# Layer 1's mixer works on an input that is not normalized: rstd moves into the Gelus, half of v into Strassen's products, and the FFNs' rstd is laid out later

## The chip, the core and the metric

The kernel runs on one core of a Trainium2 chip. The metric is the device time of one execution in microseconds. A core has five engines that run side by side, each with its own queue in order: TensorE (matmuls; the profile calls it PE, and its loads of the stationary operand PEld), VectorE (DVE), ScalarE (ACT), GpSimd (POOL) and SyncE (SP), which issues DMAs here. Matmuls write into PSUM, which has eight banks of 512 float32 columns; VectorE and ScalarE move results from there to SBUF. Engines wait for one another on semaphores.

## The reference, cut to what matters

A decoder trunk of two layers on 512 tokens with 1024 channels, in float32. In layer 0 the mixer is a gated short convolution and a causal pooling; in layer 1 it is a chunked spatial gating:

```python
xn = rms_norm(h, norm_mix[1])                # h * rstd(token) * gain(channel)
proj = gelu(xn @ w_in_odd)                   # 1024 -> 2048, exact Gelu
u, v = proj[..., :1024], proj[..., 1024:]
mix = chunked_spatial_gating(u, v, ...)      # vn = rms_norm(v); gate over 128 positions; u * gate
h = h + mix @ w_out_odd
```

After each mixer comes a gated convolutional FFN of width 2816: `g` and `up` are products of the normalized input, `g` goes through a causal convolution of width 3, and `silu(g) * up` is multiplied by `w_ffn_down`. The rstd of an RMSNorm is one number per token. It is a factor of a whole row of `xn`, so it can as well be applied to the row of `xn @ w`.

## The kernel before, in words

**Numbers.** Each float32 operand is split into a high and a low half (`hi`, `lo`, type float32r), and a product is three matmuls (`mm3`, L153 to L156): hi x hi, hi x lo, lo x hi. The splits are the main work of ScalarE (`hi`, a copy) and VectorE (`lo`, the difference): `parts` for weights (L146), `halves` and `split` for others. `summed` (L136) makes `lo` with ScalarE and an accumulating DMA of POOL.

**Layout.** `h` is held in eight tiles of 128 channels x 512 tokens; `hg` are the halves of h times the gain, not yet times rstd. `Norm.rstd_cols` (L223) makes rstd with tokens on partitions: eight tiny matmuls of the sum of squares, then a root and a Newton step on VectorE and ScalarE (`inv_sqrt`). `Norm.rstd_spread` (L213) lays it out along the free axis: four transposes on TensorE (`ssr`) and a copy on ScalarE.

**Strassen.** The FFNs' `both` (L682) and layer 1's `InProducts` (L907) multiply 2 x 2 blocks with seven products for eight, in Winograd's form. `multiply` (L532) runs one product of 12 matmuls of 256 columns. Products 1, 6, 7 and 4 accumulate in one bank "a", 5 and 3 in "e", 2 in "b"; after a product of "a" ScalarE copies the state out of the bank before the next product adds to it. The token side needs sums of blocks (`t23`, `t41` in the FFNs, `sums` in the mixer), the weight side sums of raw weight blocks (`rest`, L922), each split again.

**Layer 1's mixer** (`mixer1`, L817). v is 512 + 512 columns of `w_in_odd`, u likewise. `v_group(0)` multiplies `hg` as it is with the first half of v's weights, plainly, with tokens as the stationary operand; its results get rstd as the scale of their Gelu (L965). Meanwhile rstd is made and laid out, at the hooks (3, 0) and (4, 2) of the group. With it `normalize(kp)` (L872), for four pairs of channel tiles, makes the normalized input, splits it into `hg` anew, and makes and splits the four block sums. `v_group(1)` multiplies the second half of v plainly with the normalized `hg`. `u0 = InProducts("u0", 0)` is Strassen's, with the block sums; the second half of u is plain (`in_group("u1", ...)`), and spatial gating runs along with it.

**The FFNs.** The first two columns of tiles (f = 0) are plain: `direct` (L605) runs triples `(i, j)`, i over eight channel tiles, j over two gate and two up tiles. At its hooks, `rstd_cols` is made at (3, 0) and `rstd_spread` at (4, 1) (L771 to L774). `block_sums` of the FFN (L635) is called after it in the program, then the results leave PSUM with rstd as a factor (L624). All later pairs f = 2, 4, ... go through `both`, with a half of the down projection between two of them (`STEPS`, L523).

**Order.** The order of the instructions on each engine is made by a planner: it takes ready work by priority, which is the order in the program, with its own estimates of durations, so instructions of later parts fill gaps of earlier ones. It does so on TensorE too. Instructions wrapped in `inorder` keep their place in TensorE's stream; `rstd_cols` and `rstd_spread` are. `behind` adds an order by hand. Buffers are rings: `raw` has four weight tiles, `whi` and `wlo` six each, PSUM seven banks for matmuls and one for others.

Of the kernel before, what the change touches and what calls it, by code (L numbers as in the profile page):

```python
# [32 lines left out]
def tile_trunk(ctx: ExitStack, tc: tile.TileContext, x, norm_mix, norm_ffn, final_norm,  # L33
# [486 lines left out]

    STEPS = [(0, None, [0]), (2, (0, 2, 0), [2]), (4, (0, 2, 1), [4])]  # L523
    for f in range(6, NF, 4):
        STEPS += [(f, (f - 4, f, 0), []), (f + 2, (f - 4, f, 1), [f, f + 2])]
    HALF = S // 2
    NP = NK // 2
    PAIRS = [k for i in range(NP) for k in (i, i + NP)]
# [25 lines left out]
    class Ffn:  # L554
# [211 lines left out]
        def hidden(self, f, before=lambda i, j: None):  # L766

            if f == 0:
                def first(i, j):
                    before(i, j)  # L770
                    if (i, j) == (3, 0):  # L771
                        nc.vector.tensor_copy(self.cols, self.norm.rstd_cols(inorder))
                    elif (i, j) == (4, 1):
                        self.r = self.norm.rstd_spread(inorder)  # L774

                ch = self.pair_weights([("g", 0), ("u", 0), ("g", 1), ("u", 1)])
                rest = self.direct(ch, first)
# [6 lines left out]
            def split_acts():  # L784
                for ft, row in rows:
                    self.act(ft, row)

            return split_acts

        def steps(self, half_down, before=lambda i, j: None):  # L790
            waiting = {}
            for f, part, ready in STEPS:
                waiting[f] = self.hidden(f, before)
                if part is not None:
                    half_down(*part)
                for done in ready:
                    waiting[done]()

    def ffn0(norm):
        nonlocal prm1  # L800
        with tc.tile_pool(name="f0", bufs=1) as ap:
            def sums(kp):
                return [ap.tile([P, 2, HALF], F32R, name=f"t23{i}_{kp}") for i in "hl"]

            ffn = Ffn(0, prm0, norm, ap, sums)
            def half_down(a, b, half):
                project(f"d0_{a}", w_ffn_down[0], ffn.acts, list(range(a, b)), None,
                        halves=(half,), tail=0)

            ffn.steps(half_down)  # L810
            prm1 = params1()
            nxt = Norm("m1", lambda k: prm1("mix", k))
            project("d0_last", w_ffn_down[0], ffn.acts, list(range(NF - 4, NF)), nxt)
            return nxt


    def mixer1(norm):  # L817
        w = w_in_odd[0]
        with tc.tile_pool(name="m1", bufs=1) as mp:
# [4 lines left out]
            def v_group(half, hooks):  # L824

                chunks = {}
                c0 = 1024 + half * 512
                for kp in range(NP):
                    raw = wp.tile([P, 2, 512], F32, tag="raw", bufs=4, name=f"raw_v{half}_{kp}")
                    nc.sync.dma_start(raw, w[:, c0 : c0 + 512].rearrange(  # L830
                        "(h k p) c -> p h k c", h=2, p=P)[:, :, kp])
                    hi, lo = parts(raw, 2, 512, f"v{half}_{kp}")
                    chunks[kp], chunks[kp + NP] = (hi[:, 0], lo[:, 0]), (hi[:, 1], lo[:, 1])
                banks = {}
                head = NK - 2
                for i, j in ([(i, j) for i in range(head) for j in range(NT)]
                             + [(i, j) for j in range(NT) for i in range(head, NK)]):
                    if (i, j) in hooks:
                        hooks[i, j]()
                    k, cs = PAIRS[i], slice(j * P, (j + 1) * P)  # L840
                    if j not in banks:
                        banks[j] = mm_bank(f"v{half}_{j}")
                    mm3(banks[j], (hg[k][0][:, cs], hg[k][1][:, cs]), chunks[k],
                        i == 0, i == NK - 1)
                return banks

            r = []
            banks = v_group(0, {(3, 0): lambda: norm.rstd_cols(inorder),
                                (4, 2): lambda: r.append(norm.rstd_spread(inorder))})

            work2 = [mp.tile([P, 2, S], F32, tag="v", bufs=4, name=f"nx{i}") for i in range(4)]
            both = mp.tile([P, 4, S], F32, tag="u", bufs=2, name="nx4")
            work2 += [both[:, :2], both[:, 2:]] * 2
            v = [mp.tile([P, D], F32, tag="v", bufs=4, name=f"v{t}") for t in range(NT)]
            ssv = mp.tile([P, 4, PAD], F32, name="ssv")[:, :, :NT]

            def v_square(half, t):
# [11 lines left out]
                nc.scalar.activation(dst[0], src, AF.Copy)  # L869
                nc.vector.tensor_tensor(dst[1], src, dst[0].bitcast(F32), ALU.subtract)  # L870

            def normalize(kp):  # L872
                x, t = work2[2 * kp], work2[2 * kp + 1]
                for i, k in enumerate((kp, kp + NP)):
                    nc.vector.scalar_tensor_tensor(x[:, i, :], h[k], prm1("mix", k), r[0],
                                                   op0=ALU.mult, op1=ALU.mult)
# [5 lines left out]
                nc.vector.tensor_tensor(t[:, 0, :], a21, a22, ALU.add)  # L882
# [18 lines left out]
            class InProducts:  # L901
# [31 lines left out]
                def run(self, out_, done):  # L933
                    banks = ({}, {})
                    e = {}
                    for i, product in ((0, 1), (1, 1), (0, 2), (1, 2), (0, 6), (1, 6), (0, 5),
                                       (0, 7), (1, 5), (1, 7), (0, 4), (0, 3), (1, 4), (1, 3)):
                        hi, lo = self.stat[product]
                        ps = multiply(banks[i], f"{self.name}_{i}", product, tokens(product, i),
                                      lambda kp: (hi[:, kp, :], lo[:, kp, :]))  # L940
                        c = {1: (0, 0), 2: (0, 0), 6: (0, 1), 3: (0, 1), 7: (1, 1), 5: (1, 1),
                             4: (1, 0)}[product]
                        dst = out_(i + 2 * c[0])[:, c[1] * HALF : (c[1] + 1) * HALF]
                        if product in (1, 6):
                            nc.scalar.copy(dst, ps)
                        elif product == 5:
                            e[i] = ps
                        elif product == 7:
                            nc.scalar.copy(dst, ps)
                            nc.vector.tensor_tensor(dst, e[i], dst, ALU.add)  # L950
                            nc.scalar.activation(dst, dst, AF.Gelu)
                        elif product == 4:
                            nc.scalar.activation(dst, ps, AF.Gelu)
                            done(i + 2)
                        else:
                            nc.vector.tensor_tensor(dst, ps, dst, ALU.add)
                        if product == 3:
                            row = out_(i)
                            nc.scalar.activation(row, row, AF.Gelu)
                            done(i)  # L960

            for kp in range(NP):
                normalize(kp)
            for t in range(NT):
                nc.scalar.activation(v[t][:, :512], banks[t], AF.Gelu,  # L965
                                     scale=norm.cols[:, t : t + 1])
                v_square(0, t)
            banks = v_group(1, {})
            for t in range(NT):
                nc.scalar.activation(v[t][:, 512:], banks[t], AF.Gelu)  # L970
                v_square(1, t)
            u0 = InProducts("u0", 0)
            u0.plain()

# [86 lines left out]
                        spatial(j + 4)  # L1061

            def u1_done(t, ps):
                nc.scalar.activation(u[1][:, t, :], ps, AF.Gelu)
# [16 lines left out]
    def ffn1(norm):  # L1081
        with tc.tile_pool(name="f1", bufs=1) as ap:
# [96 lines left out]
            ffn.steps(half_down, before)  # L1179
            last_down(NF - 4, NF)  # L1180

    def down(name, ks, pieces, lhs, rhs, on_done):
# [42 lines left out]
```

## Time and profile before

| | |
|---|---|
| median of 3 runs | 994.0 us (993.97 to 995.07) |
| profiled execution | 993.98 us, its span 992.2 us |
| granted TensorE clock | 0.999 |
| busy: PE, PEld, DVE, ACT, POOL | 980.7, 880.9, 769.4, 544.6, 99.1 us |
| matmuls | 6049 |
| DMA | 125.1 MB |

In the rows of the profile a line like `L543 PE MATMUL u_0a<-whi_u,hgh` names the line of the kernel, the engine, the operation, and the tiles written and read, numbers left out of most names. In rows in order of time the first two columns are the start and the duration in microseconds; a bracket at the end is the engine's idle time before the instruction and what ended it. Durations of matmuls hold their drain, so they overlap; what a matmul costs in a stream is the distance from its start to the next one's. A row of a waits view is: who waited, for whom, microseconds in total, times, longest. In the groups by line the figures are the count, busy time and mean nanoseconds, and then the engine's idle time ahead of them.

Layer 1's mixer starts at 494.2 us with the first half of v; the second half starts at 517.4, u0 at 539.1, and u1 with the spatial gating at 559.4. The FFNs' plain parts are at about 139 to 172 us and 636 to 663 us.

### The profile page before, as it was taken

The numbers are of one execution on the slowest core, as the hardware profiler recorded it, in microseconds if no ns is written. First come the engines' busy times: TensorE is split into PE (matmuls) and PEld (weight loads), VectorE is DVE, ScalarE is ACT, GpSimd is POOL, SyncE is SP. The second block draws the span as 40 slices with busy tenths as digits, with TensorE's granted clock in tenths as the row PEclk, the third lists the DMA queues.
The fourth block names the chain that finished last, engine by engine and source line by source line (L and its number), as shares of the span: only waits on it lengthen the run. The fifth ranks groups of instructions, "written<-read, shape, count | busy, mean of one in ns | idle before, by whom it ended". The sixth has DMA issues, their size and how long they took to land.

```text
span 992.2 us, 15316 instructions
## 1 busy us (share of the span) xinstructions
PE 980.7 (99%) x6049; PEld 880.9 (89%) x6049; DVE 769.4 (78%) x1174; ACT 544.6 (55%) x816; POOL 99.1 (10%) x117
## 2 busy tenths in 40 slices
PE   9999999999999999999999999999999999999997
PEld 6788887999999999999888988889999999999986
DVE  5897458998788887886787665589987779777776
ACT  5623346765465654655568734576655456554544
POOL 2142022100000000000300001210000000000000
PEclk9999999999999999999999999999999999999999
DMA  7442225555455454553433513265554555455512
GB/s 246 130 149 85 86 86 127 127 140 158 129 149 133 129 143 129 149 128 114 128 99 84 174 61 103 57 138 129 149 159 132 136 142 145 122 135 137 139 54 85
DMA packets 85251, 125.10 MB, mean 126 GB/s; under 512 B 4180, under 2 KB 56124, under 8 KB 85180
## 3 DMA queue, kind: packets, MB, share of 16 engines
q1 hardware_dynamic: 76204, 98.24, 31.8%
q0 software_dynamic: 7056, 23.60, 13.1%
q10 hardware_dynamic: 1920, 2.30, 0.7%
q8 instruction: 47, 0.77, 0.3%
q14 instruction: 24, 0.20, 0.1%
HBM read 98.42 MB, written 2.10 MB: 101 GB/s over the span
## 4 chain that ended last, share of the span: by engine, by line
PE 92%; DVE 2%; ACT 1%; issue 1%; DMA 0%; POOL 0%; ACTq 0%; DVEq 0%
PE dn L154 4%; PE dn L156 4%; PE dn L155 4%; PE d L155 3%; PE d L154 3%; PE d L156 3%; PE v L154 1%; PE oo L154 1%; PE oo L155 1%; PE v L155 1%; PE v L156 1%; PE oo L156 1%; PE oe L155 1%; PE oe L154 1%; PE oe L156 1%; PE g_2a L543 1%
## 5 line engine op out<-in xcount | busy, mean ns | idle before, releaser
L154 PE MATMUL dn<-whi_dn,a_hi 128*128 128x512 f32 (+1 forms) x180 | 69.3, 385 | 0.0
L155 PE MATMUL dn<-wlo_dn,a_hi 128*128 128x512 f32 (+1 forms) x180 | 69.3, 385 | 0.0
L156 PE MATMUL dn<-whi_dn,a_lo 128*128 128x512 f32 (+1 forms) x180 | 69.2, 384 | 0.0
L577 DVE SCALAR_TENSOR_TENSOR c<-rows,prm,c 128x512 f32<-128x512 f32 x88 | 63.6, 743 | 0.8 <-ACT c L575 0.8
L154 PE MATMUL d<-a_hi,whi_d 128*128 128x512 f32 x144 | 56.1, 390 | 0.0
L155 PE MATMUL d<-a_lo,whi_d 128*128 128x512 f32 x144 | 56.1, 390 | 0.0
L156 PE MATMUL d<-a_hi,wlo_d 128*128 128x512 f32 x144 | 56.0, 389 | 0.0
L141 POOL DMA_DIRECT2D wlo_g<-raw_g x20 | 17.2, 859 | 385.6 <-ACT wlo_g L140 328.1
L150 DVE TENSOR_TENSOR wlo_dn<-raw_dn,whi_dn 128x1024 fp32r<-128x1024 f32 x22 | 26.9, 1224 | 26.2 <-ACT whi_dn L149 26.1
L680 DVE TENSOR_TENSOR wlo_s34u<-s34u,whi_s34u 128x1024 fp32r<-128x1024 f32 x20 | 24.5, 1225 | 26.9 <-ACT whi_s34u L679 26.9
L1104 DVE SCALAR_TENSOR_TENSOR y<-dn,small,y 128x512 f32<-128x512 f32 (+1 forms) x49 | 33.8, 734 | 9.1 <-PE dn L156 9.1
L156 PEld LDWEIGHTS dn<-whi_dn,a_lo 128*128 128x128 f32 x180 | 33.8, 188 | 7.0 <-DVE a_lo L263 0.2
L154 PEld LDWEIGHTS dn<-whi_dn,a_hi 128*128 128x128 f32 x180 | 33.9, 188 | 6.4
L155 PEld LDWEIGHTS dn<-wlo_dn,a_hi 128*128 128x128 f32 x180 | 33.9, 188 | 6.4
L143 ACT ACTIVATE whi_u<-raw_u 128x1024 fp32r<-128x1024 f32 x21 | 22.1, 1054 | 30.7 <-PE d L155 16.5
L150 DVE TENSOR_TENSOR wlo_d<-raw_d,whi_d 128x1024 fp32r<-128x1024 f32 x18 | 22.0, 1223 | 19.9 <-ACT whi_d L149 19.9
L149 ACT ACTIVATE whi_dn<-raw_dn 128x1024 fp32r<-128x1024 f32 x22 | 23.3, 1058 | 25.4 <-issue 12.6
L261 ACT ACTIVATE a_hi<-s 128x512 fp32r<-128x512 f32 x44 | 27.3, 625 | 17.9 <-PE dn L155 12.3
L585 ACT ACTIVATE s<-c,prm 128x512 f32<-128x512 f32 x44 | 31.2, 714 | 9.1 <-DVE c L577 9.0
L199 ACT ACTIVATE hgh<-h,prm 128x512 fp32r<-128x512 f32 x24 | 17.3, 722 | 33.3 <-DVE h L310 33.2
L141 POOL DMA_DIRECT2D wlo_u<-raw_u x21 | 18.1, 861 | 169.4 <-ACT wlo_u L140 122.1
L210 POOL TENSOR_TENSOR ssq_f<-ssq_f,sq_f 128x512 f32<-128x512 f32 x14 | 19.7, 1411 | 144.1 <-ACT sq_f L209 109.2
(1386 smaller groups left out, 3638.5 us busy)
## 6 DMA issues: line engine op xcount, KB each, us to landing
raw_g<-in_w_ffn_gate_dram SPq DMA_DIRECT2D x40, 512.0 KB, 3.8
raw_u<-in_w_ffn_up_dram SPq DMA_DIRECT2D x40, 512.0 KB, 3.8
raw_dn<-in_w_ffn_down_dram SPq DMA_DIRECT2D x22, 512.0 KB, 3.6
wlo_u<-raw_u POOLq DMA_DIRECT2D x21, 512.0 KB, 5.6
wlo_g<-raw_g POOLq DMA_DIRECT2D x20, 512.0 KB, 4.7
raw_d<-in_w_ffn_down_dram SPq DMA_DIRECT2D x18, 512.0 KB, 3.7
raw_oe<-in_w_out_even_dram SPq DMA_DIRECT2D x8, 512.0 KB, 3.6
raw_v<-in_w_in_odd_dram SPq DMA_DIRECT2D x8, 512.0 KB, 4.4
```

Source lines behind the costliest of these rows:

```text
L141: nc.gpsimd.dma_start(lo, raw, accum_op=ALU.add)
L143: behind(nc.scalar.activation(hi, raw, AF.Copy), first)
L149: behind(nc.scalar.activation(hi, raw, AF.Copy), after[1])
L150: behind(nc.vector.tensor_tensor(lo, raw, hi.bitcast(F32), ALU.subtract), after[0])
L154: nc.tensor.matmul(ps, lhs[0], rhs[0], start=start, stop=False)
L155: nc.tensor.matmul(ps, lhs[0], rhs[1], start=False, stop=False)
L156: nc.tensor.matmul(ps, lhs[1], rhs[0], start=False, stop=stop)
L261: nc.scalar.activation(hi, src, AF.Copy, scale=scale)
L577: nc.vector.scalar_tensor_tensor(c, t[:, i : S + i], prm("cf", i * NF + ft), c, op0=ALU.mult, op1=ALU.add)
L585: nc.scalar.activation(s, c, AF.Silu, bias=self.prm("bf", ft))
L680: nc.vector.tensor_tensor(lo, src, hi.bitcast(F32), ALU.subtract)
L1104: nc.vector.scalar_tensor_tensor(dst, ps, ffn.cols[:, t : t + 1], dst, op0=ALU.mult, op1=ALU.add)
```

## The change

Three edits. In layer 1's mixer the input is never normalized: `normalize` becomes `block_sums`, which makes the four block sums from h and the gain alone (as the FFN's own does) and leaves `hg` as it was; there is no `rstd_spread`; `rstd_cols` is at hook (4, 0) for (3, 0); and every Gelu of v and u takes the token's rstd as its scale. The second half of v becomes an `InProducts` like u0, at columns 1536 and up. In the FFNs `rstd_spread` goes from hook (4, 1) to (6, 0) of `direct`. The rewriting of `STEPS`, `steps` and `split_acts` issues the splits of the FFN's results at the same places as before.

```diff
-    STEPS = [(0, None, [0]), (2, (0, 2, 0), [2]), (4, (0, 2, 1), [4])]
+    STEPS = [(0, None, True), (2, (0, 2, 0), True), (4, (0, 2, 1), True)]
     for f in range(6, NF, 4):
-        STEPS += [(f, (f - 4, f, 0), []), (f + 2, (f - 4, f, 1), [f, f + 2])]
+        STEPS += [(f, (f - 4, f, 0), False), (f + 2, (f - 4, f, 1), f + 4 < NF)]
...
                     if (i, j) == (3, 0):
                         nc.vector.tensor_copy(self.cols, self.norm.rstd_cols(inorder))
-                    elif (i, j) == (4, 1):
+                    elif (i, j) == (6, 0):
                         self.r = self.norm.rstd_spread(inorder)
...
-            r = []
-            banks = v_group(0, {(3, 0): lambda: norm.rstd_cols(inorder),
-                                (4, 2): lambda: r.append(norm.rstd_spread(inorder))})
-
-            work2 = [mp.tile([P, 2, S], F32, tag="v", bufs=4, name=f"nx{i}") for i in range(4)]
-            both = mp.tile([P, 4, S], F32, tag="u", bufs=2, name="nx4")
-            work2 += [both[:, :2], both[:, 2:]] * 2
-            v = [mp.tile([P, D], F32, tag="v", bufs=4, name=f"v{t}") for t in range(NT)]
+            banks = v_group(0, {(4, 0): lambda: norm.rstd_cols(inorder)})
...
-            def normalize(kp):
-                x, t = work2[2 * kp], work2[2 * kp + 1]
-                for i, k in enumerate((kp, kp + NP)):
-                    nc.vector.scalar_tensor_tensor(x[:, i, :], h[k], prm1("mix", k), r[0],
-                                                   op0=ALU.mult, op1=ALU.mult)
-                halves(hg[kp], x[:, 0, :])
-                halves(hg[kp + NP], x[:, 1, :])
-                t = t.rearrange("p a (b c) -> p (a b) c", b=2)
-                a11, a21 = x[:, 0, :HALF], x[:, 0, HALF:]
-                a12, a22 = x[:, 1, :HALF], x[:, 1, HALF:]
-                nc.vector.tensor_tensor(t[:, 0, :], a21, a22, ALU.add)
+            def block_sums(kp):
+                t = mp.tile([P, 4, HALF], F32, tag="v", bufs=4, name=f"nx{kp}")
+                g1, h1 = prm1("mix", kp + NP), h[kp + NP]
+                a11, a21 = t[:, 2, :], t[:, 3, :]
+                nc.scalar.activation(t[:, 2:, :], h[kp].rearrange("p (a b) -> p a b", a=2),
+                                     AF.Copy, scale=prm1("mix", kp))
+                nc.vector.scalar_tensor_tensor(t[:, 0, :], h1[:, HALF:], g1, a21, op0=ALU.mult,
+                                               op1=ALU.add)
                 nc.vector.tensor_tensor(t[:, 1, :], t[:, 0, :], a11, ALU.subtract)
-                nc.vector.tensor_tensor(t[:, 2, :], a11, a21, ALU.subtract)
-                nc.vector.tensor_tensor(t[:, 3, :], a12, t[:, 1, :], ALU.subtract)
+                nc.vector.tensor_tensor(a11, a11, a21, ALU.subtract)
+                nc.vector.scalar_tensor_tensor(a21, h1[:, :HALF], g1, t[:, 1, :], op0=ALU.mult,
+                                               op1=ALU.subtract)
                 halves([x[:, kp % 2] for x in sums[kp // 2]], t)
...
-                            nc.scalar.activation(dst, dst, AF.Gelu)
+                            gelu(dst, dst, i + 2)
                         elif product == 4:
-                            nc.scalar.activation(dst, ps, AF.Gelu)
+                            gelu(dst, ps, i + 2)
...
+            def gelu(dst, src, t):
+                nc.scalar.activation(dst, src, AF.Gelu, scale=norm.cols[:, t : t + 1])
+
             for kp in range(NP):
-                normalize(kp)
+                block_sums(kp)
+            v = [mp.tile([P, D], F32, tag="v", bufs=4, name=f"v{t}") for t in range(NT)]
             for t in range(NT):
-                nc.scalar.activation(v[t][:, :512], banks[t], AF.Gelu,
-                                     scale=norm.cols[:, t : t + 1])
+                gelu(v[t][:, :512], banks[t], t)
                 v_square(0, t)
-            banks = v_group(1, {})
-            for t in range(NT):
-                nc.scalar.activation(v[t][:, 512:], banks[t], AF.Gelu)
-                v_square(1, t)
+            v1 = InProducts("v1", 1536)
+            v1.plain()
+            v1.rest()
+            v1.run(lambda t: v[t][:, 512:], lambda t: v_square(1, t))
             u0 = InProducts("u0", 0)
             u0.plain()
```

More of the change, by code (lines that the diff above doesn't have):

```diff
@@ L782, in hidden, with split_acts @@
                 rows = self.both(f)
[L784 to L788, printed above, removed]
+            return rows
         def steps(self, half_down, before=lambda i, j: None):
-            waiting = {}
+            rows = []
             for f, part, ready in STEPS:
-                waiting[f] = self.hidden(f, before)
+                rows += self.hidden(f, before)
                 if part is not None:
                     half_down(*part)
-                for done in ready:
-                    waiting[done]()
+                if ready:
+                    self.split_acts(rows)
+                    rows = []
+            return rows
+        def split_acts(self, rows):
+            for ft, row in rows:
+                self.act(ft, row)
     def ffn0(norm):
@@ L808, in half_down @@
                         halves=(half,), tail=0)
-            ffn.steps(half_down)
+            ffn.split_acts(ffn.steps(half_down))
             prm1 = params1()
@@ L958, in run @@
                             row = out_(i)
-                            nc.scalar.activation(row, row, AF.Gelu)
+                            gelu(row, row, i)
                             done(i)
+            def gelu(dst, src, t):
+                nc.scalar.activation(dst, src, AF.Gelu, scale=norm.cols[:, t : t + 1])
             for kp in range(NP):
-                normalize(kp)
+                block_sums(kp)
+            v = [mp.tile([P, D], F32, tag="v", bufs=4, name=f"v{t}") for t in range(NT)]
             for t in range(NT):
-                nc.scalar.activation(v[t][:, :512], banks[t], AF.Gelu,
-                                     scale=norm.cols[:, t : t + 1])
+                gelu(v[t][:, :512], banks[t], t)
                 v_square(0, t)
-            banks = v_group(1, {})
-            for t in range(NT):
-                nc.scalar.activation(v[t][:, 512:], banks[t], AF.Gelu)
-                v_square(1, t)
+            v1 = InProducts("v1", 1536)
+            v1.plain()
+            v1.rest()
+            v1.run(lambda t: v[t][:, 512:], lambda t: v_square(1, t))
             u0 = InProducts("u0", 0)
@@ L1063, in u1_done @@
             def u1_done(t, ps):
-                nc.scalar.activation(u[1][:, t, :], ps, AF.Gelu)
+                gelu(u[1][:, t, :], ps, t)
             u[1] = mp.tile([P, NT, S], F32, tag="u", bufs=2, name="u1")
@@ L1177, in last_down @@
                 down(f"dn{a}", list(range(a, b)), pieces, lhs, rhs, done)
-            ffn.steps(half_down, before)
+            ffn.split_acts(ffn.steps(half_down, before))
             last_down(NF - 4, NF)
```

## The prediction

> **What bounds the kernel now.** I read the profile's totals first, then the chain of work that ended last, then TensorE's waits, and only then the three stages that the change touches, by their instructions in order of time.
>
> ```profile
> span 992.2 us, 15316 instructions
> PE 980.7 (99%) x6049; PEld 880.9 (89%) x6049; DVE 769.4 (78%) x1174; ACT 544.6 (55%) x816; POOL 99.1 (10%) x117
> PE 92%; DVE 2%; ACT 1%; issue 1%; DMA 0%; POOL 0%; ACTq 0%; DVEq 0%
> ```
>
> TensorE is busy for 99% of the span and makes up 92% of the chain. So the time is the sum of the matmuls' pitches plus the places where TensorE stands, and an edit on VectorE (DVE) or ScalarE (ACT) counts only where it makes TensorE stand. All of TensorE's waits that the waits view lists are three:
>
> ```profile
> PE ssr_f L217 <- DVE rc_f0c L251: 2.3, 1, 2.3
> PE clock L62 <- DVE idle L57: 1.3, 1, 1.3
> PE ssr_f L217 <- DVE rc_f1c L251: 0.8, 1, 0.8
> ```
>
> The middle one is the start of the program. The others are the laying out of rstd (four transposes, `ssr_f`) in the two FFNs, which the change moves. The profiled execution took 993.98 us, 1.8 beside its span; the median of the runs is 994.0, so the sum can be taken off either. About 0.2% (2 us) is what a measurement of this kernel can tell from no change.
>
> **Part 1: the second half of v in Strassen's products.** TensorE's instructions in order of time give the price of both forms. The first row below begins the plain second half of v (517.38), the next is where u0 begins, which has block products already, and the last is where u1 begins.
>
> ```profile
> 517.38 0.39 PE L154 MATMUL v<-whi_v,hgh 128*128 128x512 f32 x1
> 539.14 0.28 PE L543 MATMUL u_0a<-whi_u,hgh 128*128 128x256 f32 x1
> 559.35 0.40 PE L154 MATMUL u<-whi_u,hgh 128*128 128x512 f32 x1
> ```
>
> Plain: 8 blocks of the 1024 inputs x 4 token tiles x 3 partial products = 96 matmuls of 512 columns in 539.14 - 517.38 = 21.76 us, 226.7 ns each. Strassen: 7 products x 2 token tiles x 4 x 3 = 168 matmuls of 256 columns in 559.35 - 539.14 = 20.21 us, 120.3 ns each. The stationary operand is a token tile in both and the new v1 runs through the same code as u0. Gain **1.55 us**: an eighth of the columns goes, and some two fifths of that are eaten by the higher cost per column of the shorter matmul (0.47 against 0.44 ns).
>
> [...]
>
> What v1 costs beside TensorE, and what pays for it, from the groups of instructions by line in 494 to 560 us and, for forms that only other stages have, single instructions of the FFN and of u0:
>
> ```profile
> L875 DVE SCALAR_TENSOR_TENSOR nx<-h,prm,rstd_m 128x512 f32<-128x512 f32 x8 | 5.7, 746 | 0.0
> L870 DVE TENSOR_TENSOR hgl<-nx,hgh 128x512 fp32r<-128x512 f32 x8 | 5.1, 684 | 0.0
> L870 DVE TENSOR_TENSOR s<-nx,s 128x1024 fp32r<-128x1024 f32 x4 | 4.9, 1222 | 0.2 <-ACT s L869 0.2
> L882 DVE TENSOR_TENSOR nx<-nx 128x256 f32<-128x256 f32 x4 | 1.7, 419 | 0.0
> L869 ACT ACTIVATE hgh<-nx 128x512 fp32r<-128x512 f32 x8 | 4.8, 630 | 1.1 <-DVE nx L875 1.0
> L149 ACT ACTIVATE whi_u<-raw_u 128x1024 fp32r<-128x1024 f32 x10 | 10.6, 1061 | 3.0 <-DVE raw_u L927 1.3 <-PE v L156 1.3 <-PE u_1a L543 0.4
> ...
> 152.22 0.47 DVE L646 SCALAR_TENSOR_TENSOR t<-h,prm,t 128x256 f32<-128x256 f32 x1
> 157.20 0.73 ACT L640 ACTIVATE t<-h,prm 128x512 f32<-128x512 f32 x1
> 544.69 0.35 ACT L945 COPY u<-u_0a 128x256 f32<-128x256 f32 x1
> ```
>
> VectorE: `normalize` goes, 5.7 + 5.1 + 4.9 + 16 small sums of 0.42 = 22.4 us; `block_sums` comes, per pair two multiply-adds of 256 columns (0.47 each), two sums of 0.42 and one 1.22, 12.0 for four pairs: 10.4 saved. v1 adds four sums of raw blocks and six low halves for four, 6 x 1.22 = 7.3, and six additions out of PSUM of 0.42: 9.8 spent. Net -0.6. ScalarE: 4.8 for `hgh` and 0.6 for the copy of rstd go, four scaled copies of 0.73 come; eight weight activations for four (+4.2), six copies out of PSUM of 0.35 (+2.1), six Gelus for four (+0.5). Net +4.3 us, the Gelus an estimate. POOL gets one more accumulating DMA (`summed`), SP the same four 512 KB loads. The cover is the room in the stage:
>
> ```profile
> 494.00:517.40 23.40, 23.40 (x111) 19.48 (x110) 18.50 (x30) 14.07 (x19) 2.69 (x2) 1.00 0.36 113
> 517.40:539.10 21.70, 21.70 (x97) 18.00 (x96) 19.64 (x28) 17.21 (x31) 0.88 (x1) 1.00 0.20 46
> ```
>
> Columns: window, length, busy PE, PEld, DVE, ACT, POOL, clock, DMA. DVE has 38.1 of 45.1 us, ACT 31.3 (35.6 after). Order matters more than the sum: `block_sums` need no rstd, so they start when h is complete (about 494) and not after rstd. From 494.5 VectorE has the sums (12.0), three low halves (3.7), two raw sums (2.4) and some 2 us of rest to do before product 6 of v1 at 517 + 4 x 1.44 = 522.7: 20 us in 28. Cost **0**; if that cover went, each us of lateness beyond the 8 would be a us of TensorE. The weight buffers (six) are a ring: v1 takes seven where it took four, and by the order in which they are asked for u0's second split gets the buffer that v1's product 6 frees at about 524.6, while u0 wants it at about 539. Also 0.
>
> **Part 2: layer 1's mixer lays out no rstd.** Four transposes go out of TensorE's stream:
>
> ```profile
> 507.39 0.60 PE L217 MATMUL ssr_m<-ident,rc_m1c 128*128 128x128 f32 x4
> 507.75 0.48 PE L154 MATMUL v<-whi_v,hgh 128*128 128x512 f32 x1
> 508.06 0.39 PE L155 MATMUL v<-wlo_v,hgh 128*128 128x512 f32 x1
> ```
>
> 507.75 - 507.39 = 0.36, and the matmul behind them has 0.31 for 0.23: **0.44 us** gained. `rstd_cols` moves from (3, 0) to (4, 0), 2.7 us later (four triples); its first reader is then v0's Gelu, at 512.8 at the soonest, when v0's first bank is done: 0. The Gelus take a column as their scale for a constant: no more instructions. The new `STEPS` and `split_acts` issue the same work in the same order: 0.
>
> **Part 3: the FFNs' rstd laid out later.** The hook goes from (4, 1) to (6, 0), seven triples or 7 x 0.68 = 4.8 us further on. Layer 0, in order of time:
>
> ```profile
> 158.78 0.39 PE L156 MATMUL gu<-hgh,wlo_g 128*128 128x512 f32 x1
> 161.44 0.62 PE L217 MATMUL ssr_f<-ident,rc_f0c 128*128 128x128 f32 x4 [2.27 <-DVE rc_f0c L251]
> 160.12 0.69 DVE L699 TENSOR_TENSOR s12g<-raw_g,raw_g 128x512 f32<-128x512 f32 x1 [1.44 <-issue]
> 161.14 0.15 DVE L251 SCALAR_TENSOR_TENSOR rc_f0c<-ms_f0c,rc_f0c 128x4 f32<-128x4 f32 x1
> 170.31 1.37 DVE L624 TENSOR_TENSOR rows<-gu,rstd_f 128x512 f32<-128x512 f32 x2 [0.38 <-PE gu L156]
> 172.47 2.74 DVE L577 SCALAR_TENSOR_TENSOR c<-rows,prm,c 128x512 f32<-128x512 f32 x4 [0.79 <-ACT c L575]
> 175.12 1.22 DVE L680 TENSOR_TENSOR wlo_s12u<-s12u,whi_s12u 128x1024 fp32r<-128x1024 f32 x1
> 176.70 0.28 PE L543 MATMUL u_2e<-t,wlo_s12u 128*128 128x256 f32 x1
> ```
>
> TensorE stood 161.44 - 158.78 - 0.23 = 2.43 us, since rc was queued on VectorE behind `s12g`. At (6, 0) TensorE comes at about 163.8, after rc (161.3): that wait goes. What is late next: VectorE. `wlo_s12u` ended at 176.34 and TensorE read it at 176.70; it would now ask 2.4 us sooner, and VectorE had stood only 0.38 + 0.79 = 1.17 us between rc and there, both times for something that TensorE's progress sets. In the old order the gain is thus about 1.2 and a new wait of about 1.2 appears at `u_2e`; if the planner puts `g_2b` (weights ready) ahead of `u_2e`, it is up to 2.43. Ends 0 and 2.43; I take **1.2**, by the idle rows. The copy of rstd on ScalarE comes by 166, its readers from 168: 0.
>
> Layer 1:
>
> ```profile
> 651.47 0.39 PE L155 MATMUL gu<-hgl,whi_g 128*128 128x512 f32 x1
> 652.70 0.62 PE L217 MATMUL ssr_f<-ident,rc_f1c 128*128 128x128 f32 x4 [0.84 <-DVE rc_f1c L251]
> 651.79 0.69 DVE L699 TENSOR_TENSOR s12g<-raw_g,raw_g 128x512 f32<-128x512 f32 x1
> 666.25 1.22 DVE L680 TENSOR_TENSOR wlo_s12u<-s12u,whi_s12u 128x1024 fp32r<-128x1024 f32 x1
> 667.52 0.39 PE L543 MATMUL u_2e<-t,wlo_s12u 128*128 128x256 f32 x1
> ```
>
> The wait is 1.23 - 0.23 = 1.00 us. Here `wlo_s12u` (done 667.47) was already 0.05 us ahead of its reader, and VectorE ran to it from 651.79 without a pause, so in the old order the whole 1.00 moves to `u_2e`. Ends 0 and 1.00; I take **0.3**, nearer the row that says 0.
>
> **Sum:** 1.55 + 0.44 + 1.2 + 0.3 = 3.5 us off 994.0: **990.5 us**, span 988.7.
>
> **The rivals.** (a) The FFNs' waits go altogether, because the planner fills in other products: 1.55 + 0.44 + 2.43 + 1.00 = 5.4, 988.6 us. For it: before, layer 0 had `g_2b` split in seven and five matmuls around another product, so the planner does fill. Against it: nothing says that its estimates see VectorE as late as it is. (b) The FFN part gives nothing, both waits moving to `u_2e` whole: 2.0 off, 992.0, on the edge of "same". (c) Slower, by ScalarE's queue. Product 6 accumulates onto product 1's bank, so it waits until ScalarE has copied product 1 out. u0 shows how near that is:
>
> ```profile
> 545.13 0.36 PE L543 MATMUL u_0a<-whi_u,s 128*128 128x256 f32 x1
> 516.69 1.27 ACT L965 ACTIVATE v<-v,rc_m1c 128x512 f32<-128x512 f32 x2
> 522.81 0.64 ACT L859 ACTIVATE sqv<-v 128x512 f32<-128x512 f32 x1
> ```
>
> The copy quoted in part 1 (544.69) ended at 545.04, product 6 began 0.09 later: no slack, although product 1 had ended four us before. In v1 the copies stand behind v0's Gelus and squares, which ran from 516.69 to 523.5. If these, and three weight activations (3.2), stay ahead of the copies, product 6 begins at about 527 for 522.7, 4.4 lost, and u0 might lose 1.5 as its start moves up: 990.5 + 5.9 = 996.4. It decides for slower from 5.5 us of such waits. Against it: v0's banks are done from 512.8 on, and without `normalize` ScalarE can take the first Gelus there. (d) Shorter matmuls lose by a pitch that doesn't fall with their columns: from 129.5 ns (21.76 / 168) part 1's first gain is gone, and at the 226.7 ns of 512 columns, the far end, v1 takes 38.1 us and the kernel 990.5 + 17.9 = 1008.4. u0's 120.3 ns speak squarely against it. [...]
>
> **How the numbers follow.** Forecast (989.4 to 991.6) 0.43; (a) 0.22; (b) 0.18, about half of it within 0.2%; (c) 0.12; (d) 0.01; 0.04 for small waits that cancel the gain, at 994. Faster 0.43 + 0.22 + 0.09 = 0.74, same 0.09 + 0.04 = 0.13, slower 0.13. Likeliest 990.5, with its own range 989.4 to 991.6; the range of 8 in 10 goes from (a)'s 988.2 to 994.4 and leaves out most of (c).
>
> **What would show it.** Right: no wait on `rc_f0c` or `rc_f1c`; v1's 168 matmuls at 120 ns, about 20.2 us from its first to u0's first; no `ssr_m` after 500 us; DVE near 767, ACT near 549 us busy; a wait of about a us at `u_2e` in layer 0 on `wlo_s12u`, or `g_2b` ahead of it. Wrong: TensorE waiting at `v1`'s or `u0`'s product 6 on a copy at L945, or on the block sums or on a low half of v1; or the planner, which sees other times now, leaving gaps in places that the change does not touch.

## The result, and the profile after

The changed kernel takes 991.43 us (median of 7 runs, 991.09 to 992.12) beside 994.93 for the kernel before in the same session (7 runs, 993.97 to 995.63): a ratio of 0.997, 95% interval 0.996 to 0.998. The forecast was 990.5, worked out from an execution of 993.98. Executions of the kernel before come in two groups, near 994.0 and near 995.4, with different granted clocks (last section), so I compare the two traces, both taken at a mean clock of 0.999: 993.98 against 991.47, 2.5 us, where the forecast said 3.5.

From the page of the changed kernel: span, busy times, chain, and then all of TensorE's waits.

```profile
span 989.4 us, 15461 instructions
PE 978.7 (99%) x6117; PEld 882.7 (89%) x6117; DVE 770.3 (78%) x1170; ACT 549.6 (56%) x823; POOL 101.0 (10%) x118
PE 85%; DVE 6%; ACT 3%; issue 1%; DMA 0%; ACTq 0%; POOL 0%; DVEq 0%
```

```profile
PE u_2e L543 <- DVE wlo_s12u L680: 1.9, 2, 0.9
PE clock L62 <- DVE idle L57: 1.3, 1, 1.3
PE v_0a L543 <- ACT v L938: 0.2, 1, 0.2
PE g_2a L543 <- ACT rows L733: 0.2, 1, 0.2
```

Both waits on rc are gone, and two waits on VectorE's `wlo_s12u`, one in each FFN, have come. They are on the path: VectorE's share of the chain is 6%, where it was 2%. The instructions of TensorE in order of time show the ends of the stages:

```profile
174.00 0.40 PE L543 MATMUL u_2e<-t,whi_s12u 128*128 128x256 f32 x2
175.35 0.39 PE L543 MATMUL u_2e<-t,wlo_s12u 128*128 128x256 f32 x1 [0.95 <-DVE wlo_s12u L680]
177.81 0.38 PE L543 MATMUL g_2a<-t23h,whi_s12g 128*128 128x256 f32 x1 [0.16 <-ACT rows L733]
...
515.89 0.28 PE L543 MATMUL v_0a<-whi_v,hgh 128*128 128x256 f32 x1
521.52 0.28 PE L543 MATMUL v_1b<-whi_v,hgl 128*128 128x256 f32 x1
522.03 0.39 PE L543 MATMUL v_0a<-whi_v,s 128*128 128x256 f32 x1 [0.24 <-ACT v L938]
536.53 0.28 PE L543 MATMUL u_0a<-whi_u,hgh 128*128 128x256 f32 x1
556.81 0.40 PE L154 MATMUL u<-whi_u,hgh 128*128 128x512 f32 x1
...
663.37 0.40 PE L543 MATMUL u_2e<-t,whi_s12u 128*128 128x256 f32 x2
664.68 0.39 PE L543 MATMUL u_2e<-t,wlo_s12u 128*128 128x256 f32 x1 [0.91 <-DVE wlo_s12u L680]
```

From the first matmuls of each stage in such lists, the stages that differ (us; "plain" is f = 0, "f = 2" runs to the down projection's first matmul). Layer 0's plain part begins at 146.5 us, not at about 139; layer 1's is counted from the transposes of h that stand between its first products:

| Stage | before | after | difference | forecast |
|---|---|---|---|---|
| FFN 0, plain (hook) | 25.66 | 23.18 | -2.48 | -2.43 |
| FFN 0, f = 2 | 20.35 | 21.77 | +1.42 | +1.2 |
| mixer 1, first half of v | 23.18 | 22.71 | -0.47 | -0.44 |
| mixer 1, second half of v | 21.76 | 20.64 | -1.12 | -1.55 |
| u0 | 20.21 | 20.28 | +0.07 | 0 |
| u1 with the spatial gating | 30.39 | 30.08 | -0.31 | 0 |
| FFN 1, plain (hook) | 27.80 | 26.79 | -1.01 | -1.00 |
| FFN 1, f = 2 | 20.58 | 21.61 | +1.03 | +0.7 |

All others agree within 0.02 us. The sum is -2.9, as the span has it (992.2 to 989.4); the time around the span, 1.8 us before and 2.1 after, gave back 0.3.

### The profile page after: what moved, and what is told of

The parts are those of the page before. It is cut to its first block, busy times and chain, and to the rows that moved or that the text cites. A ratio compares the mean times of both kernels' runs of the same rounds, so it can differ in the third digit from the quotient of the medians.

```text
span 989.4 us, 15461 instructions
## 1 busy us (share of the span) xinstructions
PE 978.7 (99%) x6117; PEld 882.7 (89%) x6117; DVE 770.3 (78%) x1170; ACT 549.6 (56%) x823; POOL 101.0 (10%) x118
## 4 chain that ended last, share of the span: by engine, by line
PE 85%; DVE 6%; ACT 3%; issue 1%; DMA 0%; ACTq 0%; POOL 0%; DVEq 0%
PE dn L154 4%; PE dn L155 4%; PE dn L156 4%; PE d L155 3%; PE d L154 3%; PE d L156 3%; PE oo L156 1%; PE oo L154 1%; PE oo L155 1%; PE oe L156 1%; PE oe L155 1%; PE oe L154 1%; PE u_20a L543 1%; PE u_18a L543 1%; PE u_16a L543 1%
## 5 line engine op out<-in xcount | busy, mean ns | idle before, releaser
L577 DVE SCALAR_TENSOR_TENSOR c<-rows,prm,c 128x512 f32<-128x512 f32 x88 | 63.8, 746 | 0.2 <-ACT c L575 0.2
L585 ACT ACTIVATE s<-c,prm 128x512 f32<-128x512 f32 x44 | 31.2, 714 | 9.3 <-DVE c L577 9.3
```

The lines of the kernel that those rows point to most:

```text
L577: nc.vector.scalar_tensor_tensor(c, t[:, i : S + i], prm("cf", i * NF + ft), c, op0=ALU.mult, op1=ALU.add)
L585: nc.scalar.activation(s, c, AF.Silu, bias=self.prm("bf", ft))
```

## The experiments

Times below are medians; "stage" times are read from TensorE's first matmuls as above. "f = 2" and "plain" are the stages of the table.

**One part alone, one part undone.** First the changed kernel with the old hook, then the kernel before with the new hook, then the changed kernel with a plain second half of v.

```diff
-                    elif (i, j) == (6, 0):
+                    elif (i, j) == (4, 1):
```

> The kernel after with the FFNs' rstd_spread back at hook (4, 1); all else as after. Theory (the prediction's terms): part 3 is worth 1.0 us, all of it in layer 0, so the span is 989.4 + 1.0 = 990.4 us; the waits at ssr_f come back (2.4 us in layer 0 counted as pitch, 1.0 in layer 1), and the waits of 1.1 us each at u_2e on wlo_s12u go. Rival: the wait only changes its place in both layers, and what layer 0 gained came from the new order elsewhere; then the span is 989.4 as after. Second rival: part 3 was worth its whole 3.4 us and something else lost 2.4; then 992.8.

```diff
 # in the kernel before
-                    elif (i, j) == (4, 1):
+                    elif (i, j) == (6, 0):
```

> The kernel before with only the FFNs' rstd_spread moved to hook (6, 0). Theory: 992.2 - 1.0 = 991.2 us of span, with waits of 1.1 us at u_2e in both layers, and nothing changed in layer 1's mixer (23.2, 21.8 and 20.2 us for the two halves of v and u0). Rival (the gain is not additive, it needs the mixer's change): 992.2.

```diff
-            v1 = InProducts("v1", 1536)
-            v1.plain()
-            v1.rest()
-            v1.run(lambda t: v[t][:, 512:], lambda t: v_square(1, t))
+            banks = v_group(1, {})
+            for t in range(NT):
+                gelu(v[t][:, 512:], banks[t], t)
+                v_square(1, t)
```

> The kernel after with the second half of v plain again, on the input that is not normalized, its Gelus scaled by rstd. Theory: Strassen's products are worth what their stretch shows, 21.76 - 20.64 = 1.1 us, so the span is 989.4 + 1.1 = 990.5, v1 takes 21.8 us from its first matmul to u0's first, and the wait of 0.4 us at v1's product 6 is gone with its cause. Rival: the 0.3 us that the stretch from u1 to the output projection gained after also hangs on v1 finishing sooner; then 990.8. Second rival: leaving out normalize alone gives more than the four transposes (VectorE freer, u0 sooner); then under 990.2.

The old hook gave 992.25 us (ratio to the kernel before 0.9979, interval 0.997 to 0.9988), with layer 0 at 25.65 and 20.36 us and layer 1 at 27.82 and 20.58, as in the kernel before. So the hook is worth 1.06 us in layer 0 and nothing in layer 1, and the rest of the change the remaining 1.8.

The other two came out slower than their parts. The hook alone gave 994.92 (0.9997, 0.9988 to 1.0006): its layer 0 took 23.18 us plain and 21.84 in f = 2, as in the changed kernel, but layer 1's f = 2 took 22.56 us, 0.95 more than there. With plain v1 the time was 993.72 (0.9992, 0.9983 to 1.0001); v's second half went back to 21.76 and u0 to 20.15 us, a net worth of Strassen's form of 1.0, but layer 1's f = 2 took 24.17, 2.56 more. In both traces, VectorE's instructions show the same thing in layer 1; first the hook alone, then plain v1:

```profile
651.60 0.69 DVE L699 TENSOR_TENSOR s12g<-raw_g,raw_g 128x512 f32<-128x512 f32 x1 [0.91 <-DMA t<-t]
```

```profile
650.62 0.69 DVE L699 TENSOR_TENSOR s12g<-raw_g,raw_g 128x512 f32<-128x512 f32 x1 [0.89 <-DMA t<-t]
```

`s12g` uses the buffer "sum" (three in a ring) that held the block sums of K chunk 1, and these are read by POOL's accumulating DMA (`t<-t`, L656). That DMA landed later than in the changed kernel (5.5 and 5.4 us after its issue, where there it was 4.4), VectorE stood for 0.9 us, and TensorE's wait at `u_2e` grew from 0.91 to 1.86 us. The other 1.6 us of plain v1 are explained in the last section. This pointed to something under both the old waits and the new ones, which the prediction had passed over.

**Does another order of products help?** Product 2 of g, whose weights are ready, goes ahead of the late product for f = 2.

```diff
+            if f == 2:
+                order.remove(("g", 2))
+                order.insert(3, ("g", 2))
```

> The kernel after with, for f = 2 alone, product 2 of g asked for ahead of products 6 of g and 5 of u, so that TensorE has 1.4 us of ready work before it needs wlo_s12u. Theory A: VectorE's late wlo_s12u is the only thing that holds this stage; then both waits go (1.1 and 1.1) and the span is 989.4 - 2.2 = 987.2. Theory B: ScalarE is as late as VectorE: its copies of product 1 (L733, at 177.4 in layer 0 and 667.8 in layer 1) let product 6 start at 177.8 and 668.2 whatever the order; then the wait moves to g_2a on the copy, about 1.4 us in layer 0 and 1 us in layer 1, and the span stays at 989.4.

991.5 us (0.9967, 0.9954 to 0.9979), the same as the changed kernel. TensorE's waits:

```profile
PE g_2a L543 <- ACT rows L733: 1.7, 2, 1.3
PE clock L62 <- DVE idle L57: 1.3, 1, 1.3
PE z L420 <- ACT hgh L397: 0.7, 1, 0.7
PE u_2b L543 <- DMA wlo_u<-raw_u: 0.5, 1, 0.5
```

The wait at `u_2e` is gone and about the same time is lost elsewhere: at `g_2a` 1.3 us in layer 0 and 0.3 in layer 1, and in layer 1 another 0.5 at `u_2b`, for the low half that POOL's accumulating DMA makes. Product 6 (`g_2a`) needs ScalarE's copy of product 1, which stands behind the gate's Silus (`s`, L585) and `whi_s34u`. Filling TensorE's queue didn't help since ScalarE was next.

**Moving what stands ahead, on VectorE and ScalarE.** For f = 2, u's remaining sums are asked for after product 1 of u.

```diff
+                late = f == 2 and key == "u"
+                if late:
+                    split_s12()
+
+                def others(...):      # summed(...), s34 and its split, as before
...
+                if not late:
+                    others()
...
+                if f == 2 and (key, product) == ("u", 1):
+                    others()
```

> The changed kernel with the second FFN step of each layer (f = 2) reordered: u's remaining weight sums (rows two of its weights, and the sums s34 of products 7 and 3) are asked for only after product 1 of u, so that ScalarE's copy of product 1 of g no longer stands behind u's s34 activations, and VectorE's wlo_s12u no longer behind four convolution steps. Theory A, TensorE waits there only because of the places of these two in their queues: the waits at u_2e (0.95 us in layer 0, 0.91 in layer 1) and at g_2a (0.16) go, the stage from f = 2 to the down projection falls from 21.77 to 20.3 us in layer 0 and from 21.61 to 20.5 in layer 1, 2.5 us together: 989.0. Theory B, VectorE has too much to do between the hook and f = 2, whatever its order: the same wait turns up at the operands now made later (products 2, 7 of u), the stages stay at 21.6 to 21.8: 991.4.

989.2 us (0.9945, 0.9933 to 0.9958): theory A. `wlo_s12u` now stands ahead of the four convolution steps (L577), and f = 2 takes 20.70 us in layer 0 and 20.16 in layer 1. Seven products of twelve 120 ns matmuls for g and for u are 20.16 us, so in layer 1 nothing is left. VectorE, in layer 0, the changed kernel and then this one:

```profile
169.94 1.28 DVE L624 TENSOR_TENSOR rows<-gu,rstd_f 128x512 f32<-128x512 f32 x2
171.42 2.74 DVE L577 SCALAR_TENSOR_TENSOR c<-rows,prm,c 128x512 f32<-128x512 f32 x4 [0.20 <-ACT c L575]
174.08 1.22 DVE L680 TENSOR_TENSOR wlo_s12u<-s12u,whi_s12u 128x1024 fp32r<-128x1024 f32 x1
```

```profile
169.74 1.28 DVE L624 TENSOR_TENSOR rows<-gu,rstd_f 128x512 f32<-128x512 f32 x2
170.93 1.22 DVE L680 TENSOR_TENSOR wlo_s12u<-s12u,whi_s12u 128x1024 fp32r<-128x1024 f32 x1
172.06 2.73 DVE L577 SCALAR_TENSOR_TENSOR c<-rows,prm,c 128x512 f32<-128x512 f32 x4
```

The edit takes work out of the way in ScalarE's queue too (its copy of product 1 ends at 173.0 us, where it was 177.8), and the run doesn't separate the two. About 0.5 of the gain in layer 0 is lost again in the next stage, f = 4, to a wait of 0.24 us at `u_4e` and small ones behind it (20.65 us for 20.15).

**The copy ahead of v's product 6.** Three of v1's weight splits are asked for after product 1.

```diff
-            v1.rest()
-            v1.run(lambda t: v[t][:, 512:], lambda t: v_square(1, t))
+            v1.rest(late=True)
+            v1.run(lambda t: v[t][:, 512:], lambda t: v_square(1, t), v1.rest_late)
```

> The changed kernel with three of v1's weight splits (for products 7, 4 and 3) asked for after product 1 and not ahead of it, so that ScalarE makes its copies of product 1 ahead of them. Theory A, the 0.24 us and shorter waits at product 6 come from that queue: v1's stretch falls from 20.64 to 20.25 us and the time by 0.4, to 991.0. Theory B, the splits then come late for product 7 or 4: a wait at v_0b or v_1b takes their place, 991.4 to 992.4.

992.06 us (0.997, 0.9959 to 0.998). That is no gain on the changed kernel (991.43). v's second half fell to 20.15 us, the wait at product 6 was gone, so it had come from that queue; but u0 took 21.05 for 20.28, with this wait on the same kind of copy, one stage later:

```profile
PE u_0a L543 <- ACT u L945: 0.6, 1, 0.6
```

It is theory A's mechanism with theory B's time, and the wait that came in its place is one that I had not named: in u0, ScalarE is what ends last.

**Taking the accumulating DMA away.** The block sums of chunk 1 are split by VectorE, as those of chunks 2 and 3 are: two subtractions (0.69 us each) more for VectorE, two copies (0.6 us each) fewer for ScalarE, no DMA reading the buffer that `s12g` takes. First in layer 1 alone, on the changed kernel with plain v1 and on the kernel before.

```diff
-                if kp > 1:
+                if kp > (1 if self.layer == 0 else 0):
```

> The changed kernel with v1 as plain products (as in the run with plain v1), and with layer 1's block sums of K chunk 1 split by VectorE as chunks 2 and 3 are, and not by the accumulating DMA. Theory L, in the run with plain v1 the layer-1 FFN lost 2.56 us because the DMA that makes t's low half for chunk 1 landed late and held the buffer that s12g needs: without that DMA its stretch from f = 2 to the down projection is 21.6 us, not 24.17, and the time is that of the changed kernel and what v1's Strassen was worth (1.0), 992.4, in every run. Theory N, the late DMA goes with something else that is late: the stretch stays above 22.5, 993.7.

> The kernel before with the same edit alone: layer 1's block sums of K chunk 1 split by VectorE, not by the accumulating DMA. Its own times fall into two groups, near 994.1 and near 995.3. Theory L, the upper group is that DMA landing late: the upper group is gone, the median is 994.0 and the spread under 0.6. Theory N, it is something else: two groups 1.2 apart remain and the median is 994.9. If VectorE's two added subtractions (2 of 0.69 us) cost something, both groups move up by up to 1.4.

With plain v1: 990.97 us (0.9963, 0.995 to 0.9977), with 20.48 us in f = 2 of layer 1 for 24.17. So 0.9 us of the loss there fits the late DMA, whose row shows 0.89 us of idle time, and 1.6 is the stretch of the last section; but 20.48 is also 1.13 less than in the changed kernel itself, where no wait on the DMA was shown. There VectorE stands earlier, and for ScalarE: 5.24 us ahead of `t` (L642) at 645.21, until ScalarE's `t` (L640), which stands behind its copies of chunks 0 and 1 and of the transposed h. With the edit in both layers (below) that idle time is 0.93 us, beside 1.58 and 0.31 just ahead of the new subtractions, and `wlo_s12u` starts 29.8 us after the stage's first matmul for 31.1. So in layer 1 of the changed kernel it was most likely ScalarE's copies and not the DMA; no run takes away the one without the other. In the kernel before the same edit gave 994.89 (1.0001, 0.9992 to 1.001) and its two groups remained: there `u_2e` had no wait to lose, and the groups are not this DMA's. Theory N for that question.

Then in both layers, on the changed kernel, together with the reordered f = 2, and on the kernel before.

```diff
-                if kp > 1:
+                if kp > 0:
```

> The changed kernel, with the block sums of K chunk 1 split by VectorE in both layers, and not by the accumulating DMA. It tells what lies under the wait of the second FFN step. Theory Q (VectorE's queue runs late because something early in it waited for that DMA's end, or for ScalarE's two extra copies that feed it): layer 1's stretch from f = 2 to the down projection falls from 21.61 to 20.48 us as in the run with plain v1 and this edit, layer 0's by as much or by what its 1.2 and 1.4 us of VectorE's idle time before the hook allow, 989.2 to 990.3. Theory W (it is VectorE's amount of work): two subtractions of 0.69 us more per layer make it later, layer 0's stretch grows from 21.77 to 23.1, 992.8.

> Both edits: f = 2 reordered as in the run that asks for u's remaining sums after product 1 of u (989.2), and the block sums of K chunk 1 split by VectorE in both layers. Layer 1's stretch from f = 2 to the down projection stood at 20.16 us there, which leaves nothing to gain; in layer 0 a wait of 0.29 us at u_2a and, later, one of 0.24 at u_4e are left. Theory Q: ScalarE's saved copies (about 1.2 us in each layer) take these two away, 988.6. Theory W: 989.2, or up to 1.4 more if VectorE's two subtractions delay wlo_s12u.

> The kernel before with K chunk 1's block sums split by VectorE in both layers, nothing else changed. In the kernel before, layer 0's rc_f0c stands on VectorE behind s12g, which stands idle for 1.44 us until the accumulating DMA has landed. Theory D, that DMA is also what makes the transposes at the old place (chunk 4, second pass) wait: rc_f0c is ready at about 159.5 us and not at 161.3, the 2.4 us wait at ssr_f shrinks by 1.5 to 2.0 us, and 993.0 minus 0.5 to 1.0, that is 992.0 to 992.5, is the lower of the times seen (994.0 for the kernel before). Theory H, the wait is the hook's place alone: it stays at 2.4 us and the time at 994.0 to 994.9.

| Kernel | us | ratio to before | FFN 0: plain, f = 2 | FFN 1: plain, f = 2 |
|---|---|---|---|---|
| changed, chunk 1 by VectorE | 988.99 | 0.9942 (0.993 to 0.9955) | 23.18, 20.35 | 26.81, 20.48 |
| the same, f = 2 reordered | 988.27 | 0.9937 (0.9923 to 0.995) | 23.18, 20.15 | 26.80, 20.15 |
| before, chunk 1 by VectorE | 991.88 | 0.9968 (0.9956 to 0.998) | 24.16, 20.36 | 27.70, 20.47 |

Theory Q and theory D. VectorE, layer 0, in the changed kernel and then with chunk 1 split by VectorE (f = 2 in the program's order):

```profile
156.60 0.69 DVE L680 TENSOR_TENSOR t<-t,t 128x512 fp32r<-128x512 f32 x1 [1.23 <-ACT t L679]
160.16 0.69 DVE L699 TENSOR_TENSOR s12g<-raw_g,raw_g 128x512 f32<-128x512 f32 x1 [1.43 <-issue]
161.18 0.16 DVE L251 SCALAR_TENSOR_TENSOR rc_f0c<-ms_f0c,rc_f0c 128x4 f32<-128x4 f32 x1
```

```profile
157.21 0.68 DVE L699 TENSOR_TENSOR s12g<-raw_g,raw_g 128x512 f32<-128x512 f32 x1
159.29 0.16 DVE L251 SCALAR_TENSOR_TENSOR rc_f0c<-ms_f0c,rc_f0c 128x4 f32<-128x4 f32 x1
172.36 1.22 DVE L680 TENSOR_TENSOR wlo_s12u<-s12u,whi_s12u 128x1024 fp32r<-128x1024 f32 x1
```

Two idle times went, 1.23 us (behind ScalarE's copies) and 1.43 (the end of the DMA, which the row names "issue": the view of tile `t` gives `s12g` as what waited 1.4 us for it, and the DMA issued at 155.3 landed 4.8 us later, at 160.1), and two subtractions came: VectorE has `rc_f0c` 1.9 us and `wlo_s12u` 1.7 us sooner although it does more (0.3 of each is this execution's earlier start). With it the hook's whole gain stays. The kernel before shows the same cause under its old wait:

```profile
PE ssr_f L217 <- DVE rc_f0c L251: 0.8, 1, 0.8
PE ssr_f L217 <- DVE rc_f1c L251: 0.7, 1, 0.7
```

0.8 us for 2.3 to 2.4, without touching the hook. The edit takes the DMA and the two copies away together, so how much belongs to each was not separated. The version of both edits, at 988.27 us, is the fastest one run, 3.2 below the changed kernel.

## Why the prediction was right, and where it was off

- **What bounds the kernel.** TensorE's stream. Right: every difference is a stage of TensorE, and VectorE's and ScalarE's totals (770.3 and 549.6 us; 767 and 549 foreseen) did not matter, only their order. (By the prediction's own net of -0.6 VectorE should have come to 768.8, not 767; it gained 0.9.)
- **Strassen's v1, 1.55.** The mechanism was right and the size was too large: 1.12, and 1.05 with u0's +0.07. The pitch was right: 119.9 ns (20.15 us for 168 matmuls) in the run with v1's splits late, 120.3 foreseen. Of the missing 0.43, 0.39 is the stand at product 6: rival (c), whose mechanism came, with ScalarE's copy behind v0's Gelus and squares and behind three weight activations, as these rows say:

```profile
518.16 0.64 ACT L854 ACTIVATE sqv<-v 128x512 f32<-128x512 f32 x1
518.77 2.96 ACT L149 ACTIVATE whi_v<-raw_v 128x1024 fp32r<-128x1024 f32 x3
521.61 0.37 ACT L938 COPY v<-v_0a 128x256 f32<-128x256 f32 x1
```

  It cost 0.39 and not 4.4, since the Gelus and squares were done at 518.8 and not 523.5: without `normalize` ScalarE came to them sooner, the reason that stood against the rival. "Cost 0" for the cover was wrong by this copy; what I listed as cover was VectorE's work, and the copy is ScalarE's.
- **No `ssr_m`, 0.44.** Measured 0.47.
- **FFN 0, 1.2.** Measured 1.06, with the new wait at `u_2e`. The wait's cause was named (VectorE is late next). But I read its lateness as the amount of work ahead of `wlo_s12u`; the row of `s12g` with 1.44 us of idle was quoted, its cause "issue" passed over, and it was at the root of the old wait and, with the 1.23 us ahead of it, of the new one. So "if the planner puts `g_2b` ahead, it is up to 2.43" was wrong: `g_2b` ahead gave nothing.
- **FFN 1, 0.3.** Measured 0 (-1.01 and +1.03). The row said 0, and I took more than it said. That VectorE ran from 651.79 without a pause was right; but a pause of 5.24 us lay ahead of that, until 648.06, for ScalarE, and the working leaves it out.
- **The rest.** u1 with the spatial gating gained 0.31 us: in the kernel before one spatial product comes 0.62 us after the transposes ahead of it, in the changed kernel 0.35. That gap is absent with plain v1 too and present with the hook alone, so it goes with `normalize`; by what path is open.
- The sum of the terms was 3.5, the traces give 2.9 by stages and 2.5 by the executions' own times: off by v1's copy (0.4), FFN 1 (0.3), FFN 0 (0.1), against u1 (0.3); another 0.3 is the time around the span. That the medians lie 3.5 us apart, the number that was forecast, is luck: about one of it comes from the longer executions of the kernel before, which the prediction did not count.

## What to carry to other kernels

When a wait on TensorE names a VectorE result, follow VectorE's queue back to its last idle time before that: moving the reader later handed 1.42 of 2.48 us to the next reader in layer 0 and all of it in layer 1, and taking away what the idle rows named, here a buffer held by an accumulating DMA and ScalarE's copies that feed it, took the lateness itself away. An idle time put down to "issue" is a question, not an answer; ask which buffer the instruction writes and who reads it last. And where an engine waits near the front of a stage, two more instructions on it (1.4 us of VectorE in each FFN) can be cheaper than a transfer that saves them: the time fell by 2.4 us.

## What the runs showed of the hardware

**Behind a stand of 1.84 us the clock fell to half, which cost another 1.6.** The kernel before ran 64 more times beside the experiments: 35 took 995.0 to 996.1 us, all of them with a mean granted clock of 0.996 or 0.997, and the other 29 had a median of 994.0, 25 of them at 0.998 or 0.999. The trace with plain v1 is one of a lower clock (0.996; span 992.7 us) and shows where: TensorE in layer 1's FFN, in order of time, and the windows (length, busy PE, PEld, DVE, ACT, POOL, clock, DMA):

```profile
666.36 0.39 PE L543 MATMUL u_2e<-t,wlo_s12u 128*128 128x256 f32 x1 [1.84 <-DVE wlo_s12u L680]
668.10 0.42 PE L543 MATMUL g_2b<-hgh,wlo_g 128*128 128x256 f32 x1
668.32 0.41 PE L543 MATMUL g_2b<-hgh,whi_g 128*128 128x256 f32 x1
```

```profile
665.60:667.60 2.00, 1.24 (x10) 1.25 (x11) 1.33 (x3) 1.99 (x4) 0.00 (x0) 1.00 1.03 197
667.60:671.00 3.40, 3.40 (x18) 3.40 (x18) 3.15 (x6) 2.47 (x5) 0.00 (x0) 0.50 0.42 83
671.00:674.00 3.00, 3.00 (x27) 3.00 (x26) 0.30 (x1) 0.85 (x1) 0.00 (x0) 1.00 0.38 130
```

From 667.6 us, 1.2 us after the stand, the clock is at half (0.50) for 3.4 us, and the matmuls come at 0.21 us each for 0.12. The trace of the hook alone has a stand of 1.86 us in the same place and no such stretch (clock 1.00 from 660 to 672 us), and its f = 2 is 1.6 us shorter (22.56 for 24.17). In the trace of the kernel before TensorE is idle for 2.27 us in layer 0, and the clock behind it is 1.00 (161.5 to 180 us). So the length of a stand alone didn't decide it in these traces; what did is not shown.

The traces of the kernel before and of the changed one also end at half clock, when TensorE's work is over: from 990.3 and 986.5 us on, 5.1 and 4.2 us after its last matmul ended, for the last 1.9 and 2.9 us of the span.

Over all kernels: the five with a stand of 1.8 us or more (before, old hook, hook alone, plain v1, before with chunk 1 of layer 1 by VectorE) have executions 0.7 us or more above the median of their others at a clock of 0.996 or 0.997; the eight whose longest stand is 1.3 us or less (changed, `g_2b` ahead, reordered, v1's splits late, and the four others with chunk 1 by VectorE) had none of that clock in 39 runs, and 2 of 6 at 0.997 for the kernel before with chunk 1 by VectorE in both layers, which were not longer (992.0 and 991.84 us, the other four 991.74 to 991.93). So the change's 3.5 us between medians is 2.5 between the two traces and, by an estimate from these counts and the 1.6 us above, one of a stretch at half clock that layer 0's 2.4 us stand no longer sets off. For layer 0 itself no trace shows it. The kernel before, run once more as it is:

> The kernel before once more, for a trace of one of its longer executions. Theory G: TensorE's stand of 2.4 us in layer 0 lets the granted clock fall to half for one stretch of 3.4 us behind it, in those executions whose time is above 995; such a trace has matmul pitches of 0.43 us instead of 0.23 right behind the transposes, and layer 0's stretch from the first gate product to f = 2 is 27.2 to 27.4 us for 25.66. An execution of 994 shows 25.66 and no such stretch. Theory S, the longer executions lose their 1.2 us elsewhere: the stretch is 25.66 in both.

It took 994.0 us, with 25.64 us in the stage and no stretch at half clock, as theory G has it for an execution of 994. That doesn't tell the theories apart, and layer 0's place stays argued, from which kernels have longer executions, and is not shown.

**The accumulating DMA's end varies.** The same 256 KB `t<-t` landed early enough for `s12g` in layer 1 of the changed kernel and 0.9 us too late in two kernels that differ from it in layer 1's mixer or in v1 alone: 4.4 us from issue to landing, and 5.5 and 5.4. Why is open.
